# Softmax sums applied to the gates instead of to the exponentials, by way of DRAM, in a two-layer attention kernel

## The chip, the cores and the metric

The kernel runs on one core of one Trainium2 chip, in one launch. The metric is the device time of that launch in microseconds (us). A core has five engines that run side by side, each working through its own queue of instructions in a fixed order: TensorE (PE in the profile, with its weight loads listed apart as PEld), VectorE (DVE), ScalarE (ACT), GpSimd (POOL) and SyncE (SP), which here only issues DMA transfers. Engines wait for one another through semaphores. A result differs from "no change" here when it is more than 0.2% away.

## The reference

The reference is a trunk of two layers. Each layer normalises 512 latent tokens and 256 context tokens of width 1024, projects them with one combined weight `w_in`, runs two attention branches of eight heads of width 64, multiplies each branch by its own SiLU gate, and merges both branches. Branch A is a neighbourhood attention with a position bias, branch B a grouped-query attention. In layer 0 the context tokens are queries too (`first` in the kernel), in layer 1 only the latents are. What the change touches is this part, cut from the reference:

```python
def _attend(q, k, v):
    s = jnp.einsum('bqkgd,btkd->bkgqt', q, k).astype(jnp.float32) * (HEAD_DIM ** -0.5)
    p = jax.nn.softmax(s, axis=-1).astype(v.dtype)
    return jnp.einsum('bkgqt,btkd->bqkgd', p, v)

def _merge(a_att, b_att, a_z, b_z, g_a, g_b, w_o_a, w_o_b, w_out):
    o_a = (a_att * jax.nn.silu(a_z)) @ w_o_a
    o_b = (b_att * jax.nn.silu(b_z)) @ w_o_b
    merged = jax.nn.sigmoid(g_a) * o_a + jax.nn.sigmoid(g_b) * o_b
    return merged @ w_out
```

A softmax is an exponential divided by the sum of its row. The sum belongs to a query token, the output of a head is linear in the exponentials, and the output is multiplied by the gate of the same token. So the division can be made on the exponentials, on the head's output, or on the gate.

## The kernel before, in words

All inputs are float32. Each operand of a large product is split into a high and a low part and three products are summed, so a product of 128 by 512 by 1024 is 24 matmuls (`mm3`, lines 343 to 347). Weights come by DMA into three `raw` tiles, are copied on ACT to `whi` and subtracted on POOL or DVE to `wlo` (eight tiles of each).

A layer runs in this order: projections for branch A, branch A's attention (called NA here: neighbourhood attention), projections for branch B, branch B's attention (GQ: grouped-query attention), the merge. An attention is a loop over eight heads in `pipeline` (line 792). For head h it emits

1. the scores: q and k are staged (`stage_q`, and `stage_k` with its POOL subtraction at line 656), and for each of four tiles of 128 queries the score matmuls write PSUM (`pss`), DVE takes the row maximum (with the bias in NA, line 753; lines 685 and 899 elsewhere), ACT computes the exponential into a tile `p` and adds up its row into `r` (lines 756, 901, and 689 for context queries);
2. `softmax_tail` (line 605): a reciprocal of `r` on DVE (line 607), and the product of the whole `p` tile with 0.5/r, on DVE (line 610) for tiles 0 and 2 and the context tile, on POOL (lines 612 and 613) for tiles 1 and 3;
3. the values of head h-1: `transpose_split` (line 616) turns 128x128 blocks of `p` on TensorE into one of two PSUM tiles `pst`, ACT copies that to `pth` (line 626), DVE subtracts to `ptl` (line 627), and value matmuls add into the one PSUM tile `psv` (lines 776 to 787 in NA, 916 and 917 in GQ, 700 and 701 for context); `head_out` (line 630) adds the two halves of `psv` on ACT and DVE and multiplies the gate tile `za` or `zb` in place on POOL (line 637);
4. some pieces of `fill`: projections of gates and, in GQ, of branch A's output. They need nothing of the heads around them, so they give TensorE work while a head's softmax runs. In GQ all of them are emitted before the last head's values, in NA a ninth is left for after them.

Rows of the gate tile `za` (`zb`) hold channels: chunk j of the four has heads 2j on partitions 0 to 63 and 2j+1 on partitions 64 to 127, and tokens along the free axis. The factor 0.5 of the softmax belongs to the gate, which is kept as twice its SiLU.

`p` tiles come from a pool of 7 (NA, layer 0), 8 (NA, layer 1) or 10 (GQ) tiles, `NP_NA` and `NP_GQ`. Besides, both attentions of layer 0 and GQ of layer 1 have steps on DVE that work for a later modulation (`ada_steps`, line 223), a few per tile.

The order in which instructions stand on each engine is not that of the source: the program is built with a scheduler that follows the source's order where it can and moves an instruction ahead where its model of the engines says that the engine would idle. Only where `add_manual_dep` ties an instruction to the one emitted before it is this order kept. All DMA transfers of the kernel stand in one queue, SP's: one that waits holds up all behind it.

After GQ, branch B's gate tile is split again (`hilo`, line 516) and multiplied with `w_o_b`: chunks 0 to 2 early (`early`, line 928, one POOL subtraction each at line 520 into `gbl`), chunk 3 after the last head (line 948).

Of the kernel before, what the change touches and what calls it, by code (L numbers as in the profile page):

```python
# [28 lines left out]
NA_POOL = (1, 3)  # L29
GQ_POOL = (1, 3)  # L30
# [17 lines left out]
def hybrid_kernel(es: ExitStack, tc, x, ctx, cvec, w_ada, w_ada0, small, gvec, w_in, w_o_a, w_o_b, w_out,  # L48
                  bias_int, bias_edge, rope, ident_d, out):
    nc = tc.nc  # L50
# [46 lines left out]

    x0, ctx0 = x[0], ctx[0]
# [5 lines left out]
    cd = drp.tile([16, 128], F32, name="cd")  # L104
    gs = [drp.tile([128, 4, NTOK], F32, name=f"gs{c}") for c in range(4)]
# [95 lines left out]
    def ada_steps(l, tiles, halves, nv, pool):  # L201
# [13 lines left out]
        def dot(h, i, v):  # L215
            if v == 0:
                load_tile(h, i)
            w = cb["w"]
            o = w if v == nv - 1 else pool.tile([128, 512], BF16, tag="junk", name=nm("junk"), bufs=1)
            ins = nc.cur_bb.bb.instructions  # L220
            before = next(j for j in reversed(ins) if j.engine == mybir.EngineType.DVE)
            n = len(ins)
            V.tensor_tensor_reduce(o, w, cb[h][:, v, :], 1.0, 0.0, ALU.mult, ALU.add, asum[:, i, h, v:v + 1])
            for j in nc.cur_bb.bb.instructions[n:]:
                if j.engine == mybir.EngineType.DVE:
                    tc.add_manual_dep(j, before.name, mybir.DependencyInfo(
                        mybir.DependencyClass.NoSync, mybir.DependencyReason.DATA), reason="program order")
# [229 lines left out]
    def layer(l, hx, nxt, mid):  # L457
# [146 lines left out]
        if True:  # L604
            def softmax_tail(p, n, r, pieces, eng=None):

                V.reciprocal(r, r)  # L607
                for i, (c0, c1) in enumerate(pieces):
                    if eng is None:
                        V.tensor_scalar(p[:, c0:c1], p[:, c0:c1], r[:, i:i + 1], 0.5, ALU.mult, ALU.mult)  # L610
                    else:
                        G.tensor_scalar(r[:, i:i + 1], r[:, i:i + 1], 0.5, None, ALU.mult)  # L612
                        G.tensor_tensor(p[:, c0:c1], p[:, c0:c1],  # L613
                                        r[:, i:i + 1].to_broadcast([128, c1 - c0]), ALU.mult)
# [63 lines left out]
            def ctx_scores(q, kh, kl):  # L678
# [8 lines left out]
                r = sp.tile([128, 2], F32, tag="r", name=nm("r"), bufs=8)  # L687
                for i in range(2):
                    S.activation(p[:, 256 * i:256 * i + 256], pss[:, 256 * i:256 * i + 256], AF.Exp,
                                 bias=mx[:, i:i + 1], accum_out=r[:, i:i + 1])  # L690
                softmax_tail(p, 512, r, [(0, 256), (256, 512)])
# [41 lines left out]
            def na_scores(h, q, kh, kl):  # L733
# [354 lines left out]
```

## Time and profile before

| what | value |
|---|---|
| time, median of 3 runs | 1183.07 us (1182.45 to 1184.28) |
| the profiled execution, its own time | 1181.47 us |
| its span, first to last instruction | 1179.7 us |
| mean granted TensorE clock | 0.998 |
| NA of layer 0, then of layer 1, by the first and the last of their matmuls | 158 to 320 us, 805 to 917 us |
| GQ of layer 0, then of layer 1, likewise | 410 to 600 us, 968 to 1112 us |

The profile lists for each engine the busy time, and for each group of instructions the source line, the engine, the operation, the tile written and the tiles read (`ptl<-pst,pth`), the shape, the count, the busy time, the mean duration and the idle time of the engine just ahead of the group with what ended it. A matmul's duration is modelled and longer than the distance between two matmuls that follow each other, so a TensorE that is shown busy can still lose a little time.

### The profile page before, as it was taken

What the parts mean: (1) busy time and instruction counts of PE and PEld (TensorE: products, weight loads), DVE (VectorE), ACT (ScalarE), POOL (GpSimd) and SP (SyncE); (2) the same over time, 40 slices, a digit from 0 to 9 for tenths busy, and PEclk for the clock granted to TensorE, in tenths of its full rate; (3) what the DMA queues carried; (4) which work ended last, traced back from release to release, by engine and by line L of the source; (5) the groups of instructions that cost most, each with busy time, mean ns of one, the idle gap of its engine ahead of it and who ended that gap; (6) DMA issues with size and microseconds to landing.
All of it is one profiled execution on the core that took longest, in us unless ns stands there. A gap on an engine that the chain in (4) does not pass through costs nothing. (4 is left out here: it accounts for less than half of the span.)

```text
span 1179.7 us, 17337 instructions
## 1 busy us (share of the span) xinstructions
PE 1130.4 (96%) x6078; PEld 948.8 (80%) x6078; DVE 812.2 (69%) x1506; ACT 575.0 (49%) x1171; POOL 508.3 (43%) x463
## 2 busy tenths in 40 slices
PE   4999999899999999999999999999999999999898
PEld 3688877788897888878788887887888878877686
DVE  4476689987474499978683455339786757798573
ACT  4353255466453355566430355436666545756531
POOL 2362444453267233453420225336553764654311
PEclk9999999999999999999999999999999999999999
DMA  9544323422152343371170322312322525452133
GB/s 315 188 144 135 111 80 111 120 82 61 55 157 87 118 143 112 72 263 38 41 192 18 125 90 72 116 43 88 119 78 71 159 80 183 142 179 98 37 127 96
DMA packets 88128, 134.05 MB, mean 114 GB/s; under 512 B 10756, under 2 KB 52712, under 8 KB 86376
## 3 DMA queue, kind: packets, MB, share of 16 engines
q1 hardware_dynamic: 88040, 132.94, 36.1%
q8 instruction: 48, 0.79, 0.3%
q14 instruction: 40, 0.33, 0.1%
HBM read 115.58 MB, written 17.32 MB: 113 GB/s over the span
## 5 line engine op out<-in xcount | busy, mean ns | idle before, releaser
L627 DVE TENSOR_TENSOR ptl<-pst,pth 128x512 fp32r<-128x512 f32 (+1 forms) x176 | 115.9, 672 | 40.7 <-ACT pth L626 39.6
L332 POOL TENSOR_TENSOR wlo<-raw,whi 128x512 fp32r<-128x512 f32 x64 | 91.7, 1435 | 119.8 <-ACT whi L330 99.6
L345 PE MATMUL psf<-hx,whi 128*128 128x512 f32 (+1 forms) x368 | 138.9, 378 | 1.1 <-DVE za L480 1.0
L346 PE MATMUL psf<-hx,whi 128*128 128x512 f32 (+1 forms) x368 | 138.3, 376 | 0.0
L347 PE MATMUL psf<-hx,wlo 128*128 128x512 f32 (+1 forms) x368 | 137.9, 375 | 0.0
L626 ACT CAST pth<-pst 128x512 fp32r<-128x512 f32 (+1 forms) x176 | 98.8, 578 | 80.0 <-PE pst L623 56.2
L345 PE MATMUL psx<-whi,hx 128*128 128x512 f32 (+1 forms) x368 | 134.9, 374 | 0.0
L346 PE MATMUL psx<-wlo,hx 128*128 128x512 f32 (+1 forms) x368 | 134.4, 369 | 0.0
L347 PE MATMUL psx<-whi,hx 128*128 128x512 f32 (+1 forms) x368 | 133.4, 370 | 0.0
L318 POOL TENSOR_TENSOR wlo<-raw,whi 128x512 fp32r<-128x512 f32 (+1 forms) x52 | 68.1, 1310 | 146.1 <-ACT whi L315 123.6
L315 ACT CAST whi<-raw 128x512 fp32r<-128x512 f32 (+1 forms) x112 | 64.8, 591 | 111.2 <-PE psx L347 39.6
L330 ACT CAST whi<-raw 128x512 fp32r<-128x512 f32 x128 | 78.1, 621 | 56.2 <-DMA raw<-in_w_in_dram 41.0
L623 PE MATMUL pst<-ident,p 128*128 128x128 f32 x640 | 100.4, 273 | 3.6 <-POOL p L613 1.2
L623 PEld LDWEIGHTS pst<-ident,p 128*128 128x128 f32 x640 | 77.8, 140 | 16.8 <-POOL p L613 1.6
L613 POOL TENSOR_TENSOR p<-p,r 128x512 f32<-128x512 f32 (+1 forms) x64 | 86.6, 1353 | 5.2
L332 DVE TENSOR_TENSOR wlo<-raw,whi 128x512 fp32r<-128x512 f32 x64 | 63.4, 991 | 36.0 <-ACT whi L330 35.5
L612 POOL TENSOR_SCALAR r<-r 128x1 f32<-128x1 f32 x64 | 24.2, 378 | 135.9 <-DVE r L607 123.9
L345 PEld LDWEIGHTS psf<-hx,whi 128*128 128x128 f32 x368 | 69.5, 189 | 12.9 <-DVE za L480 1.7
L347 PEld LDWEIGHTS psx<-whi,hx 128*128 128x128 f32 x368 | 69.4, 189 | 12.0 <-issue 0.8
L345 PEld LDWEIGHTS psx<-whi,hx 128*128 128x128 f32 x368 | 70.0, 191 | 11.1
L346 PEld LDWEIGHTS psx<-wlo,hx 128*128 128x128 f32 x368 | 69.6, 189 | 11.3
L347 PEld LDWEIGHTS psf<-hx,wlo 128*128 128x128 f32 x368 | 69.4, 188 | 11.6
(239 smaller groups left out, 3049.4 us busy)
## 6 DMA issues: line engine op xcount, KB each, us to landing
raw<-in_w_in_dram SPq DMA_DIRECT2D x160, 256.0 KB, 2.9
rawb<-in_w_ada_dram SPq DMA_DIRECT2D x64, 256.0 KB, 2.7
gs<-zt SPq DMA_DIRECT2D x32, 256.0 KB, 2.6
raw<-in_w_out_dram SPq DMA_DIRECT2D x32, 256.0 KB, 2.7
tg<-gs SPq DMA_DIRECT2D x4, 1536.0 KB, 7.8
rawx<-in_w_ada_dram SPq DMA_DIRECT2D x4, 1024.0 KB, 11.9
rawy<-in_w_ada_dram SPq DMA_DIRECT2D x4, 1024.0 KB, 12.7
raw<-in_w_o_a_dram SPq DMA_DIRECT2D x16, 256.0 KB, 3.2
```

The lines of the kernel that those rows point to most:

```text
L315: S.copy(hi[:, :n], raw[:, :n])
L318: e.tensor_tensor(lo[:, :n], raw[:, :n], F(hi[:, :n]), ALU.subtract)
L330: S.copy(hi, raw)
L332: lo_eng(i).tensor_tensor(lo, raw, F(hi), ALU.subtract)
L345: T.matmul(ps, lhs[0], rhs[0], start=first, stop=False)
L346: T.matmul(ps, lhs[0], rhs[1], start=False, stop=False)
L347: T.matmul(ps, lhs[1], rhs[0], start=False, stop=last)
L612: G.tensor_scalar(r[:, i:i + 1], r[:, i:i + 1], 0.5, None, ALU.mult)
L613: G.tensor_tensor(p[:, c0:c1], p[:, c0:c1], r[:, i:i + 1].to_broadcast([128, c1 - c0]), ALU.mult)
L623: T.transpose(pt[:, c0:c0 + 128], src, ident)
L626: S.copy(hi[:, n0:n1], pt[:, n0:n1])
L627: V.tensor_tensor(lo[:, n0:n1], pt[:, n0:n1], F(hi[:, n0:n1]), ALU.subtract)
```

## The change: what it does

The exponentials are no longer divided. ACT still adds up each row, now into one tile `r` for a pair of heads: column pairs (query tile, head of the pair), 12 columns in layer 0, where the two context tiles count, and 8 in layer 1. After the odd head of a pair, `invert` doubles the sums and takes their reciprocal on DVE, and `sums_out` turns the 128x12 tile on TensorE into 12 rows of 128 in a `pst` tile, copies these on ACT into a `p` tile, and writes them to DRAM (`rd`). During the next head, `normalise` reads the rows back, each spread over the 64 partitions of its head (two transfers, one for each half of the partitions), into one or two `p` tiles, and multiplies chunk j of the gate tile with them on POOL. In NA the tile is 512 wide, so in layer 0 there are two such tiles, and the latents' part is multiplied in two pieces, because its first query tile is made of two pieces of 64 tokens. For the last pair this stands ahead of the values of head 7. The new helper `behind` ties what it emits to the instruction emitted last on the same engine; the writes of the sums and the first three `normalise` of an attention are emitted through it, so that the scheduler does not move them ahead of what the source has before them. `softmax_tail` and the two constants that chose its engine go.

```diff
+    def behind(fn):
+        ins = nc.cur_bb.bb.instructions
+        n, last = len(ins), {}
+        for i in ins[::-1]:
+            last.setdefault(i.engine, i.name)
+            if len(last) == 5:
+                break
+        fn()
+        for i in nc.cur_bb.bb.instructions[n:]:
+            if i.engine in last:
+                tc.add_manual_dep(i, last[i.engine], mybir.DependencyInfo(
+                    mybir.DependencyClass.NoSync, mybir.DependencyReason.DATA), reason="program order")
+            last[i.engine] = i.name
...
+    rd = [drp.tile([12, 128], F32, name=f"rd{i}") for i in range(4)]
...
-            def softmax_tail(p, n, r, pieces, eng=None):
-                V.reciprocal(r, r)
-                for i, (c0, c1) in enumerate(pieces):
-                    if eng is None:
-                        V.tensor_scalar(p[:, c0:c1], p[:, c0:c1], r[:, i:i + 1], 0.5, ALU.mult, ALU.mult)
+            def sums_tile():
+                return sp.tile([128, 6, 2], F32, tag="r", name=nm("r"), bufs=3)
+
+            def invert(r):
+                n = 6 if first else 4
+                V.tensor_scalar(r[:, 0:n], r[:, 0:n], 2.0, None, ALU.mult)
+                V.reciprocal(r[:, 0:n], r[:, 0:n])
+
+            def sums_out(j, r):
+                n = 12 if first else 8
+                pt = psw(128, "t")
+                T.transpose(pt[0:n], r[:, 0:n // 2].rearrange("p j e -> p (j e)"), ident)
+                row = p_tile()[:, 0:128]
+                S.copy(row[0:n], pt[0:n])
+                behind(lambda: nc.sync.dma_start(rd[j][0:n], row[0:n]))
+
+            def normalise(j, z, perm):
+                zv = z.rearrange("p (f n) -> p f n", f=4)[:, j]
+                n = 6 if first else 4
+                w = min(att["w"] // 128, n)
+                for j0 in range(0, n, w):
+                    j1 = min(j0 + w, n)
+                    rb = p_tile()[:, 0:128 * (j1 - j0)]
+                    for e in range(2):
+                        nc.sync.dma_start(rb[64 * e:64 * e + 64].rearrange("p (j q) -> p j q", q=128),
+                                          rd[j].rearrange("(j e) q -> e j q", e=2)[e:e + 1, j0:j1]
+                                          .to_broadcast([64, j1 - j0, 128]))
+                    if perm and j0 == 0:
+                        zp = zv[:, 0:512].rearrange("p (s n) -> p s n", n=64)[:, 0:8:7]
+                        G.tensor_tensor(zp, zp, rb[:, 0:128].rearrange("p (s n) -> p s n", n=64), ALU.mult)
+                        G.tensor_tensor(zv[:, 64:448], zv[:, 64:448], rb[:, 128:512], ALU.mult)
                     else:
-                        G.tensor_scalar(r[:, i:i + 1], r[:, i:i + 1], 0.5, None, ALU.mult)
-                        G.tensor_tensor(p[:, c0:c1], p[:, c0:c1],
-                                        r[:, i:i + 1].to_broadcast([128, c1 - c0]), ALU.mult)
+                        zp = zv[:, 128 * j0:128 * j1]
+                        G.tensor_tensor(zp, zp, rb, ALU.mult)
...
                     S.activation(p[:, :512], p[:, :512], AF.Exp, bias=mx[:, 0:1], scale=-1.0,
-                                 accum_out=r[:, 0:1])
-                    softmax_tail(p, 512, r[:, 0:1], [(0, 512)], G if i in NA_POOL else None)
+                                 accum_out=r[:, i, h % 2:h % 2 + 1])
...
+            def pair_sums(h):
+                if h % 2 == 0:
+                    att["r"] = sums_tile()
+                return att["r"]
+
-            def pipeline(fill, spread, scores_of, values_of, last=None, bg=[]):
+            def pipeline(fill, spread, scores_of, values_of, z, perm, last=None, bg=[]):
...
                     if prev is not None:
                         values_of(h - 1, prev)
+                    if h % 2:
+                        invert(att["r"])
+                        sums_out(h // 2, att["r"])
+                    elif h:
+                        behind(lambda: normalise(h // 2 - 1, z, perm))
                     run(fill, len(fill) - (n - n * min(h + 1, spread) // spread))
...
                 run(bg, len(bg))
+                normalise(3, z, perm)
                 values_of(7, prev)
```

The same replacement of `softmax_tail` by a column of `r` is made in `ctx_scores` and `gq_scores`. The old inline tie in `ada_steps` now goes through `behind`.

More of the change, by code (lines that the diff above doesn't have):

```diff
@@ L219, in dot @@
             o = w if v == nv - 1 else pool.tile([128, 512], BF16, tag="junk", name=nm("junk"), bufs=1)
[L220 to L227, printed above, removed]
+            behind(lambda: V.tensor_tensor_reduce(o, w, cb[h][:, v, :], 1.0, 0.0, ALU.mult, ALU.add,
+                                                  asum[:, i, h, v:v + 1]))
         res = []
```

31 lines of the change are left out of this document (13 added, 18 removed).

## The prediction

> **What bounds the kernel now.** I read the head of the page first, then the busy time by stage, then who waits for whom on PE, then single waits on the timeline.
>
> ```profile
> span 1179.7 us, 17337 instructions
> PE 1130.4 (96%) x6078; PEld 948.8 (80%) x6078; DVE 812.2 (69%) x1506; ACT 575.0 (49%) x1171; POOL 508.3 (43%) x463
> ```
>
> TensorE is busy for 96% of the span, and none of its matmuls is removed. So the change can only buy back time in which TensorE waits, 1179.7 - 1130.4 = 49.3 us in all, and of that only what lies in the four attentions. The busy time by stage gives that part (the columns are PE, PEld, DVE, ACT and POOL, each with its count, then PE's clock, the DMA share and GB/s); the rows are NA and GQ of layer 0, then NA and GQ of layer 1:
>
> ```profile
> 158.00:320.00 162.00, 154.24 (x948) 135.67 (x949) 135.69 (x302) 90.06 (x206) 72.12 (x64) 1.00 0.29 87
> 410.00:600.00 190.00, 184.70 (x1116) 160.59 (x1115) 158.47 (x290) 107.75 (x223) 82.97 (x69) 1.00 0.40 120
> 805.00:917.00 112.00, 110.58 (x609) 94.06 (x608) 89.37 (x182) 73.09 (x156) 57.98 (x59) 1.00 0.28 89
> 968.00:1112.00 144.00, 138.31 (x708) 111.26 (x707) 114.66 (x200) 88.79 (x170) 67.52 (x58) 1.00 0.42 136
> ```
>
> TensorE idles 7.76 + 5.30 + 1.42 + 5.69 = 20.2 us there. This is a little low, because a matmul's row overlaps the next: starts 0.23 us apart, shown as 0.39 us each, so every wait hides up to 0.16 us.
>
> ```profile
> 1110.93 0.39 PE L345 MATMUL psx<-gbh,whi 128*128 128x512 f32 x1
> 1111.16 0.39 PE L346 MATMUL psx<-gbl,whi 128*128 128x512 f32 x1
> ```
>
> Some 30 such waits would add 5 us; 25 us is the ceiling. NA of layer 0 is the one place where another engine is as full as TensorE:
>
> ```profile
> 158.00:178.00 20.00, 17.94 (x108) 15.39 (x108) 18.97 (x42) 10.73 (x26) 9.19 (x7) 1.00 0.29 91
> 178.00:198.00 20.00, 19.15 (x107) 16.25 (x108) 19.87 (x49) 10.95 (x26) 8.79 (x7) 1.00 0.36 95
> 198.00:218.00 20.00, 18.43 (x119) 16.40 (x118) 19.87 (x43) 10.30 (x25) 9.83 (x8) 1.00 0.36 119
> 218.00:238.00 20.00, 16.73 (x101) 14.40 (x100) 19.43 (x41) 10.67 (x25) 9.55 (x7) 1.00 0.44 132
> 238.00:258.00 20.00, 20.00 (x128) 17.95 (x128) 18.60 (x44) 12.78 (x30) 11.91 (x10) 1.00 0.31 96
> ```
>
> DVE works 96.7 of these 100 us, and TensorE loses 7.75 us, all the idle time of that stage. Who ended it, in the same stretch (us in total, times, longest):
>
> ```profile
> PE pst L621 <- DVE ptl L627: 4.8, 2, 3.3
> PE pss L672 <- DVE za L480: 1.3, 1, 1.3
> ```
>
> **Removed.** The groups of the page (mean ns after the busy time):
>
> ```profile
> L610 DVE TENSOR_SCALAR p<-p,r 128x512 f32<-128x512 f32 (+2 forms) x96 | 64.3, 683 | 2.8 <-PE pst L623 0.5
> L607 DVE RECIPROCAL r<-r 128x1 f32<-128x1 f32 (+1 forms) x144 | 21.8, 156 | 11.9 <-ACT p L901 5.4 <-ACT p L756 4.6 <-ACT p L689 1.3
> L613 POOL TENSOR_TENSOR p<-p,r 128x512 f32<-128x512 f32 (+1 forms) x64 | 86.6, 1353 | 5.2
> L612 POOL TENSOR_SCALAR r<-r 128x1 f32<-128x1 f32 x64 | 24.2, 378 | 135.9 <-DVE r L607 123.9
> ```
>
> DVE loses 86 of 812 us, POOL 111 of 508. Nearly all of it lies beside a busy TensorE and is worth nothing by itself. Stage by stage:
>
> *NA, layer 0.* Of DVE's 96.7 us in the full stretch these two groups go:
>
> ```profile
> L610 DVE TENSOR_SCALAR p<-p,r 128x512 f32<-128x512 f32 (+1 forms) x18 | 11.4, 652 | 0.1
> L607 DVE RECIPROCAL r<-r 128x1 f32<-128x1 f32 (+1 forms) x24 | 3.6, 154 | 0.3 <-ACT p L756 0.3
> ```
>
> That is 15.0 us, twice what TensorE loses, so DVE is no longer the last on average. The wait for `za` (1.3 us) is not touched. The longest one, 3.3 us, has a cause that partly stays:
>
> ```profile
> 228.35 2.48 POOL L656 TENSOR_TENSOR kl<-ka,kh 64x768 fp32r<-64x768 f32 x1 [1.31 <-DVE kh L654]
> 229.20 2.18 DVE L223 CUSTOM_DVE_ANT_0 rawb<-rawb,cb 128x512 f32<-128x512 f32 x1
> 232.05 0.33 PE L621 MATMUL pst<-ident,p 128*128 128x128 f32 x1 [3.27 <-DVE ptl L627]
> ```
>
> The subtraction `ptl` sat behind a DVE step that took 2.18 us while POOL was working; both remain. I take 5.0 us off; bounds 0 and 9.0 (7.75 - 1.3, with 2.5 for hidden parts).
>
> *GQ, layer 0*, 5.30 us idle. Two stretches hold 4.26 of it:
>
> ```profile
> 510.00:530.00 20.00, 17.71 (x106) 14.77 (x105) 17.73 (x28) 13.14 (x28) 14.74 (x11) 1.00 0.95 365
> 570.00:590.00 20.00, 18.03 (x113) 15.22 (x112) 11.18 (x17) 7.73 (x14) 10.58 (x8) 1.00 0.13 47
> ```
>
> In the first the DMA engines are 95% busy, in the second every engine is idle half the time: neither lacks DVE. I take 1.0 us; bounds 0 and 3.0.
>
> *NA, layer 1*: 1.42 us idle; 0.5, bounds 0 and 1.4. *GQ, layer 1*: 3.16 of its 5.69 us lie at the end, where the last three heads run without fill and each group of four transposes goes through ACT and DVE before the next may start. The first and the last of ten `ptl` there:
>
> ```profile
> 1098.70 0.69 DVE L627 TENSOR_TENSOR ptl<-pst,pth 128x512 fp32r<-128x512 f32 x1 [0.49 <-ACT pth L626]
> 1109.85 0.69 DVE L627 TENSOR_TENSOR ptl<-pst,pth 128x512 fp32r<-128x512 f32 x1 [0.45 <-ACT pth L626]
> ```
>
> 11.15 us for nine, 1.24 us a group: no division stands in this chain any more, and it stays. Of the other 2.5 us I take 1.0; bounds 0 and 2.5. Saved together: 5.0 + 1.0 + 0.5 + 1.0 = 7.5 us; bounds 0 and 15.9.
>
> **Added.** Sixteen times (four pairs, two attentions, two layers): two DVE operations on 12 columns, less than the four or five reciprocals a head loses; one transpose on TensorE; one ACT copy of 12 rows; one DMA write of 4 or 6 KB; 40 DMA reads; POOL products in the place of four times as many.
>
> The transpose: a run of four takes 0.60 us, a run's first 0.27 by its group's mean, so (0.60 - 0.27) / 3 = 0.11 us each.
>
> ```profile
> L623 PE MATMUL pst<-ident,p 128*128 128x128 f32 x640 | 100.4, 273 | 3.6 <-POOL p L613 1.2 <-DVE ptl L627 1.2 <-DVE p L610 0.7
> 1108.60 0.60 PE L623 MATMUL pst<-ident,p 128*128 128x128 f32 x4
> ```
>
> Sixteen are 1.8 us; at 0.27 each, if none overlaps, 4.4. I take 1.8: fill stands around most of them. Each also borrows one of the two `pst` tiles. Under fill that is covered; in the bare ends of layer 1's attentions it costs about half a group, 0.6 us, twice: 1.2 us, from 0 to 2.5.
>
> The way through DRAM shows in no row of before. Nearest are the gates written and the `cb` rows read with a spread over partitions (first line: `zs`; second: `cb`; min, median, max); then a short copy on ACT and the issue of a transfer on SP:
>
> ```profile
> DMA to landing us min/median/max: 1.7/2.3/6.7
> DMA to landing us min/median/max: 3.1/3.6/5.1
> L635 ACT COPY ho<-psv 64x256 f32<-64x256 f32 x16 | 5.9, 368 | 10.1 <-PE psv L701 4.6 <-POOL zb L637 3.1 <-POOL za L637 2.2
> 1109.15 0.33 SPq L973 DMA_DIRECT2D xt<-xs  x1
> ```
>
> With ACT's copy (0.37 us for 256 columns), two issues of 0.33 us and the POOL product (1.35) I get 0.4 + 0.3 + 2.3 + 0.3 + 3.6 + 1.35 = 8.3 us; at the fastest rows 7.2, at the slowest 14.2. What hides it is that for three pairs of four a whole head lies between; what is queued behind it is everything on SP behind the write (weight loads, kept ahead by eight `whi`) and everything on POOL behind the product. In the built program the `kl` behind it on POOL serves a score more than a hundred matmuls later. The cover is thin for the last pair of each GQ. In layer 0 the order on POOL puts the product ahead of three `gbl`; TensorE's transpose of the sums stands right behind head 6's values:
>
> ```profile
> 571.20 0.48 PE L917 MATMUL psv<-ptl,vb 128*128 128x512 f32 x1
> 580.42 5.88 POOL L520 TENSOR_TENSOR gbl<-zb,gbh 128x768 fp32r<-128x768 f32 x3 [3.60 <-PE psf L346]
> ```
>
> From 571.4 to 580.4 are 9.0 us, against 8.3. In layer 1 six groups follow the transpose (7.4 us) and then
>
> ```profile
> 1110.60 0.50 PE L917 MATMUL psv<-ptl,vb 128*128 128x512 f32 x1 [0.23 <-DVE ptl L627]
> 1112.57 1.29 POOL L637 TENSOR_TENSOR zb<-zb,ho 64x512 f32<-64x512 f32 x1 [6.04 <-DVE ho L636]
> ```
>
> another 2.0 us until POOL needs the gate: 9.4 us, against 8.3. I cost the round trip at 0; at the slowest rows it is 14.2 - 9.0 = 5.2 us late once and 4.8 us once, 10 us. The `p` tiles that row and product borrow are given back within these 8 us; in NA of layer 0, with seven, this makes the scheduler place a score later, with fill ahead of it: nothing, as long as fill lasts.
>
> Sum: -7.5 + 1.8 + 1.2 = -4.5 us on the span, 1175.2. The profiled execution took 1181.47 against a median of 1183.07, so I carry the difference to the median: 1178.6 us.
>
> **The rivals.**
>
> *A. The round trip comes late* (slower). Place: POOL at the end of GQ in layer 0 and layer 1, where `gbl` and the last gate products queue behind a product that waits for DRAM. It costs from the point where copy, write, read and product pass 9 us; at 14.2 us it costs 10 us, so 1178.6 + 10 = 1188.6. For it: a write of `zs` took 6.7 us once. Against it: DMA is 13% busy in the stretch of layer 0's end.
>
> *B. TensorE's waits stay.* The scheduler fills the room that DVE gains: in the built order the third head of NA in layer 0 ends 36 projection matmuls earlier in TensorE's queue than before, so attention work comes denser and DVE may be last again. Then nothing is saved and 3.0 us are added: 1186.1 us. Against it: by the sixth head both orders are even, and by then DVE has shed more than the 15 us above.
>
> *C. DVE gains more than its removed rows.* DVE lines with two operands in SBUF, such as line 223, run long at times; for this line the count with its mean and then min, median and max in ns:
>
> ```profile
> L223 DVE CUSTOM_DVE_ANT_0 rawb<-rawb,cb 128x512 f32<-128x512 f32 x64 | 59.0, 922 | 1.2 <-DMA rawb<-in_w_ada_dram 0.6
> L223 DVE CUSTOM_DVE_ANT_0 rawb<-rawb,cb x64: 662/691/2183, 98.8 to 1045.3; 128x512 f32<-128x512 f32 x64
> ```
>
> The mean is 922 ns (59.0 us for 64), 231 ns over the median, and the 2.18 us row above ran beside a POOL operation. If POOL's load is the cause, losing 111 of its 508 us, less some 35 for the new products, shortens these steps by about 15%. Then the long waits of NA go too: 7.75 - 1.3 there, and half of the remaining 12.4 us elsewhere: -12.7 + 3.0 = -9.7, 1173.4 us. [...]
>
> **How the numbers follow.** The forecast 0.40, A 0.23, B 0.22, C 0.15. The bound for no change is 0.2%, 2.4 us. The forecast's own range (its savings between 3 and 11 us, 3.0 added) is 1175 to 1183. Its 0.40 goes 0.33 faster, 0.06 the same, 0.01 slower; C is all faster; A 0.03 the same, 0.20 slower; B 0.10 the same, 0.12 slower, as 3.0 lies near the bound. Faster 0.48, same 0.19, slower 0.33. The range takes in all savings at their bound less the additions (1183.1 - 15.9 + 1.8 = 1169) and A at its full price with a third of the savings lost (1191).
>
> **What would show it.** Right: PE idle in 158 to 258 us down from 7.75 to about 3, DVE there below 85%; sixteen transposes near 0.11 us; PE's order of stages unchanged; POOL's product of the last pair done before `gbl`'s turn. Wrong: PE waits for `gbl` or a last gate product at the end of GQ with a DMA as releaser (A); PE idle in NA of layer 0 still above 6 us (B); `rawb` steps near 700 ns (C). A TensorE wait for the transposed sums themselves, behind DVE's reciprocal, would be a cost that I left out.

## The result, and the profile after

The changed kernel takes 1185.69 us (median of 20 runs, 1183.18 to 1188.0), the kernel before 1183.1 us in as many runs beside it. The ratio is 1.0024 with an interval of 1.0017 to 1.0031: 2.6 us slower, where 1178.6 was forecast. The profiled execution took 1184.74 us.

The head of the page of the changed kernel:

```profile
span 1182.8 us, 17163 instructions
PE 1133.9 (96%) x6094; PEld 952.8 (81%) x6094; DVE 733.1 (62%) x1298; ACT 580.3 (49%) x1187; POOL 419.6 (35%) x363
```

DVE lost 79 us, where 86 of removed rows were counted, and POOL 89, where 111 less some 35 were. TensorE idles 1182.8 - 1133.9 = 48.9 us, before 49.3: nothing in sum. Its busy time is 3.5 us longer with the same matmuls and sixteen transposes. The busy time by stage (window and length, then PE, PEld, DVE, ACT and POOL with counts, PE's clock, DMA share, GB/s):

```profile
158.00:258.00 100.00, 98.36 (x606) 86.90 (x607) 85.44 (x181) 59.55 (x133) 32.55 (x24) 1.00 0.38 117
158.00:320.00 162.00, 160.36 (x1001) 142.29 (x1001) 116.22 (x241) 94.79 (x217) 54.09 (x46) 1.00 0.33 101
410.00:600.00 190.00, 186.70 (x1133) 163.16 (x1132) 134.79 (x227) 107.25 (x222) 59.75 (x42) 1.00 0.40 127
805.00:917.00 112.00, 108.89 (x620) 93.82 (x619) 72.78 (x144) 69.92 (x152) 42.85 (x38) 0.98 0.31 95
968.00:1112.00 144.00, 132.59 (x674) 106.02 (x673) 94.97 (x154) 83.88 (x164) 39.44 (x30) 0.99 0.42 130
```

TensorE's idle time in NA and GQ of layer 0 falls from 7.76 and 5.30 us to 1.64 and 3.30, and in NA and GQ of layer 1 rises from 1.42 and 5.69 to 3.11 and 11.41: 8.1 us won, 7.4 lost. The clock column, 1.00 in all four stages before, shows 0.98 and 0.99 in layer 1.

The same on the timeline: the last value matmuls of GQ in layer 0, of NA in layer 1 and of GQ in layer 1, first in the kernel before, then in the changed one (start, duration):

```profile
584.38 0.48 PE L917 MATMUL psv<-ptl,vb 128*128 128x512 f32 x1
...
913.32 0.25 PE L787 MATMUL psv<-ptl,va 128*128 128x192 f32 x1
```

```profile
574.97 0.48 PE L958 MATMUL psv<-ptl,vb 128*128 128x512 f32 x1
...
906.88 0.25 PE L818 MATMUL psv<-ptl,va 128*128 128x192 f32 x1
...
1113.74 0.50 PE L958 MATMUL psv<-ptl,vb 128*128 128x512 f32 x1 [0.23 <-DVE ptl L662]
```

The changed kernel is 9.4 us ahead after layer 0's attentions, 6.4 ahead after NA of layer 1, and 3.1 behind at the end of GQ of layer 1 (1113.74 against 1110.60). That last attention loses 9.6 us. Three places in the trace of the changed kernel stand out there.

*The first step on `w_ada`.* The start of GQ in layer 1 on DVE, SP, ACT and PE, then DVE and ACT at the same place before (start, duration, engine, instruction, idle time ahead of it and what ended it):

```profile
965.87 0.96 DVE L942 TENSOR_REDUCE mx<-pss 128x1 f32<-128x768 f32 x1 [0.33 <-PE pss L708]
969.43 0.84 DVE L234 CUSTOM_DVE_ANT_0 rawb<-rawb,cb 128x512 f32<-128x512 f32 x1 [2.61 <-DMA rawb<-in_w_ada_dram]
970.21 0.95 DVE L942 TENSOR_REDUCE mx<-pss 128x1 f32<-128x768 f32 x1
...
970.31 1.80 SPq L227 DMA_DIRECT2D rawb<-in_w_ada_dram  x2
972.21 1.61 SPq L335 DMA_DIRECT2D raw<-in_w_in_dram  x2
...
976.48 0.62 ACT L338 CAST whi<-raw 128x512 fp32r<-128x512 f32 x1 [3.27 <-DMA raw<-in_w_in_dram]
977.01 0.59 ACT L486 ACTIVATE zt<-psf 128x512 f32<-128x512 f32 x1
977.65 0.50 PE L353 MATMUL psf<-hx,whi 128*128 128x512 f32 x1 [3.81 <-ACT zt L486]
```

```profile
972.27 1.82 DVE L899 TENSOR_REDUCE mx<-pss 128x1 f32<-128x768 f32 x2 [0.34 <-PE pss L673]
974.29 0.17 DVE L607 RECIPROCAL r<-r 128x1 f32<-128x1 f32 x1 [0.20 <-ACT p L901]
974.49 0.62 DVE L610 TENSOR_SCALAR p<-p,r 128x768 f32<-128x768 f32 x1
975.72 1.09 DVE L223 CUSTOM_DVE_ANT_0 rawb<-rawb,cb 128x512 f32<-128x512 f32 x1 [0.61 <-DMA rawb<-in_w_ada_dram]
...
978.46 0.60 ACT L478 ACTIVATE zt<-psf 128x512 f32<-128x512 f32 x1 [0.96 <-PE psf L347]
980.86 0.62 ACT L330 CAST whi<-raw 128x512 fp32r<-128x512 f32 x1 [1.80 <-DMA raw<-in_w_in_dram]
```

The step is tied to the DVE instruction emitted last before it. Before, that was the division, which waits for the exponential: two row maxima passed ahead of it and its tile had nearly landed. Now it is the first row max. The step sits in DVE's queue 2.61 us for its transfer, with the second row max behind it. SP waits with it, for a free `rawb` buffer, so the next weight tile is asked for only at 972.21; ACT waits for that tile in front of `zt`, and TensorE for the PSUM tile that `zt` reads, 3.81 us.

SP's wait alone does not make this loss. In the kernel before SP stood still for as long (from 972.2 to 976.84), and TensorE had no such wait. Two more things differ. Two loads of `w_ada` now go ahead of the weight tile, where one did before, and ACT's cast comes 10.6 us after the first row max instead of 8.6. And `zt` now stands on ACT behind the cast that waits; before it stood ahead of it (978.46, then 980.86). Both are parts of the new order, and no run takes them apart.

*The doubling of the sums.* POOL, DVE and PE in the last heads:

```profile
1098.67 1.28 POOL L672 TENSOR_TENSOR zb<-zb,ho 64x512 f32<-64x512 f32 x1 [9.66 <-DVE ho L671]
1098.70 1.27 DVE L619 TENSOR_SCALAR r<-r 128x8 f32<-128x8 f32 x1
1100.01 0.20 DVE L620 RECIPROCAL r<-r 128x8 f32<-128x8 f32 x1
1100.24 1.29 DVE L662 TENSOR_TENSOR ptl<-pst,pth 128x512 fp32r<-128x512 f32 x2
1100.99 0.50 PE L958 MATMUL psv<-ptl,vb 128*128 128x512 f32 x1 [1.28 <-DVE ptl L662]
```

Eight columns take 1.27 us; they end when POOL's product ends, and `ptl` and TensorE wait behind them.

*The store of the gate sums.* It goes to DRAM as single numbers, and here it stands right ahead of two weight loads:

```profile
1043.63 0.37 SPq L256 DMA_DIRECT2D gd<-ag  x1
1044.09 2.12 SPq L335 DMA_DIRECT2D raw<-in_w_o_b_dram  x2
...
1056.44 0.62 ACT L338 CAST whi<-raw 128x512 fp32r<-128x512 f32 x1 [4.79 <-DMA raw<-in_w_o_b_dram]
1057.60 0.50 PE L957 MATMUL psv<-pth,vb 128*128 128x512 f32 x1 [1.46 <-ACT pth L661]
```

ACT waits 4.79 us for a weight tile that was issued by 1046.2, with `pth` behind it.

The round trip itself, for the last pair of GQ in layer 1 on SP and POOL:

```profile
1105.49 0.29 SPq L629 DMA_DIRECT2D rd<-p  x1
1106.85 1.23 SPq L640 DMA_DIRECT2D p<-rd  x2
1110.85 1.28 POOL L649 TENSOR_TENSOR zb<-zb,p 128x512 f32<-128x512 f32 x1 [1.17 <-DMA p<-rd]
```

From the write's issue to the end of the product are 6.64 us, and the last value matmuls end only after 1113.74.

### The profile page after: what moved, and what is told of

Its sections match the earlier page's. It is cut to its first block, busy times and chain, and to the rows that moved or that the text cites. A ratio compares the mean times of both kernels' runs of the same rounds, so it can differ in the third digit from the quotient of the medians.

```text
span 1182.8 us, 17163 instructions
## 1 busy us (share of the span) xinstructions
PE 1133.9 (96%) x6094; PEld 952.8 (81%) x6094; DVE 733.1 (62%) x1298; ACT 580.3 (49%) x1187; POOL 419.6 (35%) x363
## 4 chain that ended last, share of the span: by engine, by line
PE 72%; DVE 10%; POOL 6%; DMA 5%; ACT 3%; issue 3%; SPq 0%; DVEq 0%; POOLq 0%; ACTq 0%
PE psx L353 10%; PE psx L354 10%; PE psx L355 10%; PE psf L353 8%; PE psf L354 8%; PE psf L355 8%; PE pst L658 4%; DMA raw<-in_w_in_dram 2%; PE pss L707 2%; PE pss L708 2%; PE pss L783 1%; PE psv L958 1%; POOL rsb L264 1%; DVE ptl L662 1%; PE psv L957 1%
## 5 line engine op out<-in xcount | busy, mean ns | idle before, releaser
L340 POOL TENSOR_TENSOR wlo<-raw,whi 128x512 fp32r<-128x512 f32 x64 | 88.6, 1387 | 203.4 <-ACT whi L338 172.1
L340 DVE TENSOR_TENSOR wlo<-raw,whi 128x512 fp32r<-128x512 f32 x64 | 59.8, 934 | 49.6 <-ACT whi L338 49.1
L353 PEld LDWEIGHTS psf<-hx,whi 128*128 128x128 f32 x368 | 69.8, 190 | 19.1 <-ACT zt L486 5.1
L354 PEld LDWEIGHTS psf<-hx,whi 128*128 128x128 f32 x368 | 69.8, 190 | 10.5
L942 DVE TENSOR_REDUCE mx<-pss 128x1 f32<-128x768 f32 x64 | 60.6, 949 | 26.7 <-PE pss L708 26.6
```

The source lines that it names most:

```text
L340: lo_eng(i).tensor_tensor(lo, raw, F(hi), ALU.subtract)
L353: T.matmul(ps, lhs[0], rhs[0], start=first, stop=False)
L354: T.matmul(ps, lhs[0], rhs[1], start=False, stop=False)
L942: V.tensor_reduce(mx[:, 0:1], pss, AX, ALU.max, negate=True)
```

## The experiments

The theory to test (Theory 1): layer 1's loss comes from the order in its GQ, above all from the step on `w_ada` that the division no longer holds back. Its main rival: the round trip through DRAM. Each row of this table has the median of a kernel, that of the kernel before in runs beside it, and the ratio of the two, which is taken from the single runs and not exactly the quotient of the medians. "Under" and "over" before are differences of the medians.

| kernel | us | before, us | ratio (95%) |
|---|---|---|---|
| changed | 1185.69 | 1183.10 | 1.0024 (1.0017 to 1.0031) |
| e1_late_ada | 1180.33 | 1183.91 | 0.9970 (0.9958 to 0.9982) |
| e2_no_trip | 1188.49 | 1183.91 | 1.0041 (1.0027 to 1.0056) |
| e3_old_gq1 | 1178.30 | 1183.91 | 0.9947 (0.9933 to 0.9960) |
| e4_only_gq1 | 1192.77 | 1183.91 | 1.0079 (1.0067 to 1.0092) |
| e5_act_half | 1176.37 | 1183.48 | 0.9935 (0.9923 to 0.9947) |
| e6_dot_later | 1182.15 | 1183.48 | 0.9989 (0.9978 to 0.9999) |
| e7_old_l1 | 1175.20 | 1183.48 | 0.9927 (0.9915 to 0.9939) |
| e8_before_early | 1188.22 | 1183.48 | 1.0038 (1.0025 to 1.0051) |
| e9_na1_old | 1175.88 | 1183.68 | 0.9933 (0.9921 to 0.9945) |
| e10_no_turn | 1177.69 | 1183.68 | 0.9952 (0.9939 to 0.9966) |
| e11_twice | 1179.95 | 1183.68 | 0.9966 (0.9953 to 0.9978) |
| e12_only_half | 1185.00 | 1183.20 | 1.0014 (1.0003 to 1.0024) |
| e13_gd_late | 1185.10 | 1183.61 | 1.0013 (1.0000 to 1.0026) |
| e14_three | 1178.40 | 1183.61 | 0.9959 (0.9946 to 0.9971) |

**Where the loss is.** In e3 the division of before stands in GQ of layer 1 alone, in e7 in both attentions of layer 1; e4 is the reverse of e3, the new division in that one attention of the kernel before. The edit, with the condition of e3 (`name == "gq1"` in e4, `l == 0` in e7):

```diff
+                att["new"] = name != "gq1"
...
+                    if ro is not None:
+                        softmax_tail(p, 768, ro[:, 0:1], [(0, 768)], G if i in DIV_POOL else None)
```

> The changed kernel, except that layer 1's grouped attention alone divides as before (reciprocal and scale of each score tile on VectorE and GpSimd, no transposed sums, no round trip). Theory 1 (the loss arises inside that attention, and the 6 us by which the changed kernel enters it early are real): before less 5 to 8 us, 1175 to 1178, ratio 0.993 to 0.996. Theory 3 (the lead is taken back whoever divides, because a bound further on, such as the DMA traffic or the granted clock, holds the end): 1181 to 1185, ratio 0.998 to 1.002.

> The kernel before, with the new division in layer 1's grouped attention alone. Theory 1 (the loss arises inside that attention whatever the lead on entering it): before plus 6 to 10 us, 1189 to 1193, ratio 1.005 to 1.009. Theory 3 (the lead of the other three attentions is what is taken back, by a bound further on): before plus 0 to 3 us, ratio 1.000 to 1.003.

> The changed kernel in layer 0, the division of before in both attentions of layer 1. Theory 1a (layer 1's neighbourhood attention loses 2 to 3.5 us too, as its last value matmuls stand 9.4 us early at its start and 6.4 at its end): 1173 to 1176 us, ratio to before 0.991 to 0.9935. Rival (layer 1's neighbourhood attention is neutral, the 3 us are the measure's): as e3, 1177.5 to 1179.5, ratio 0.994 to 0.996.

Both e3 (5.6 us under before) and e4 (8.9 over) came out as Theory 1 has it: GQ of layer 1 costs 8 to 9 us by itself, whatever lead it is entered with. Layer 0's new division is worth 8.3 us (e7), and NA of layer 1 seemed to cost about 2.7 (e7 against e3, each by its own before; their intervals overlap).

**The step on `w_ada`, or the round trip.** e1 starts the steps in GQ of layer 1 with the second head:

```diff
                 for h in range(8):
+                    att["bg"] = bg if h >= first_bg else []
                     st = scores_of(h)
...
-            pipeline(fill, 8, gq_first, values_of(zb, gq_values), zb, False, early, bg)
+            pipeline(fill, 8, gq_first, values_of(zb, gq_values), zb, False, early, bg, 1 * l)
```

> The changed kernel, except that layer 1's grouped attention starts the steps on w_ada (rawb times cb, on VectorE) with its second head instead of its first. Theory 1 (the first such step now stands ahead of the second row max in VectorE's queue while its tile is still on the way, because the division that used to stand between them is gone; by this the PE wait of 3.8 us that ends at 977.65 comes about, and the granted clock of 0.5 from 978.8 to 982.2 behind it): that wait falls under 1 us and the dip behind it goes, 4 to 6 us in all: 1179.5 to 1182 us, against 1185.7 for the changed kernel, ratio to before 0.997 to 0.999. Theory 2 (the round trip through DRAM is what costs): the first heads have no round trip, so the time stays within 1 us of 1185.7, ratio 1.0015 to 1.003.

e2 keeps every instruction, but in GQ of layer 1 no read waits for a write of the same head pair (`trip` is set in that attention alone):

```diff
-                behind(lambda: nc.sync.dma_start(rd[j][0:n], row[0:n]))
+                behind(lambda: nc.sync.dma_start((rx if att["trip"] else rd)[j][0:n], row[0:n]))
```

> The changed kernel, except that in layer 1's grouped attention the turned sums are written to a DRAM tile that nothing reads, and the factors are read from what layer 1's neighbourhood attention left (the output is not the reference's there: it is divided by other sums). Every instruction and transfer stays, only the wait of the reads for the write is gone. Theory 1 (order of VectorE's queue in the first heads): within 1 us of the changed kernel's 1185.7, ratio to before 1.0015 to 1.003. Theory 2 (the round trip, Rival A of the prediction): 3 to 9 us less, ratio 0.995 to 0.9995.

e1 gains 6.2 us on the changed kernel (3.6 under before against 2.6 over), e2 none: it came out about 2 us above, which nobody expected and which lies at the edge of the two intervals. The round trip of that attention is not the loss. In e1's trace the wait at that place is down to 0.87 us:

```profile
973.92 0.50 PE L353 MATMUL psf<-hx,whi 128*128 128x512 f32 x1 [0.87 <-ACT zt L486]
```

**Its place in the queue, in both kernels.** e6 leaves the loads where they are and puts each step behind the next row max. e8 does the reverse to the kernel before: the step ahead of the division, nothing else.

```diff
+            def shift(h, i):
+                load_tile(h, i)
+                todo.append((h, i, 0, cb["w"]))
+                if len(todo) > 1:
+                    dot(*todo.pop(0))
...
```

```diff
                     S.activation(p, pss, AF.Exp, bias=mx[:, 0:1], accum_out=r[:, 0:1])
+                    if l == 1:
+                        run(att["bg"], att["per"])
                     softmax_tail(p, 768, r[:, 0:1], [(0, 768)], G if i in GQ_POOL else None)
                     ps_.append(p)
-                    run(att["bg"], att["per"])
+                    if l == 0:
+                        run(att["bg"], att["per"])
```

> The changed kernel, with each step on w_ada in layer 1's grouped attention put one score tile later in VectorE's order, so behind the next row max; the loads of its tiles are issued in the same heads as in the changed kernel. Theory 1 (the step's place in VectorE's queue is what costs): about what e1 gains, 1179.5 to 1182.5 us, ratio to before 0.997 to 0.9995. Rival (the traffic of these loads in the first head costs, wherever the step stands): within 1.5 us of 1185.7, ratio 1.0010 to 1.0035.

> The kernel before, with nothing changed but that in layer 1's grouped attention each step on w_ada is placed ahead of the division of its score tile instead of behind it, so that it stands behind the first row max in VectorE's order as in the changed kernel. Theory 1 (that place is what costs): before plus 3 to 6 us, 1186.5 to 1190, ratio 1.0025 to 1.005. Rival (the place costs nothing by itself; the loss needs the new division's other parts): within 1.2 us of before, ratio 0.999 to 1.001.

e8 makes the kernel before 4.7 us slower without a single part of the change, and its trace shows the row that the changed kernel has:

```profile
974.26 0.96 DVE L899 TENSOR_REDUCE mx<-pss 128x1 f32<-128x768 f32 x1 [0.34 <-PE pss L673]
977.72 0.94 DVE L223 CUSTOM_DVE_ANT_0 rawb<-rawb,cb 128x512 f32<-128x512 f32 x1 [2.50 <-DMA rawb<-in_w_ada_dram]
978.59 0.95 DVE L899 TENSOR_REDUCE mx<-pss 128x1 f32<-128x768 f32 x1
```

Where TensorE pays for it is not all the same, though. It waits 1.30 us for `zt` here (at 984.92), 1.76 for `ptl` at 1051.47, and two stretches at half clock follow in this attention, from 1052.09 and 1103.29 (see the last section). So e8 shows that the order costs, not that it always costs by one wait.

e6 gains 3.9 us of e1's 6.2 (1.3 under before against 2.6 over), at the far end of what Theory 1 gave; TensorE still waits 2.05 us at that place:

```profile
979.02 0.50 PE L366 MATMUL psf<-hx,whi 128*128 128x512 f32 x1 [2.05 <-ACT zt L499]
```

So the place in the queue is most of it. The rest, 2.3 us, e6 does not divide: the loads are still issued in the first head, and `zt` still stands behind the cast that waits.

**The doubling.** e5 is e1 without line 619; the factor goes into ACT's copy. e12 is the same edit on the changed kernel, without e1's.

```diff
-                V.tensor_scalar(r[:, 0:n], r[:, 0:n], 2.0, None, ALU.mult)
...
-                S.copy(row[0:n], pt[0:n])
+                S.activation(row[0:n], pt[0:n], AF.Identity, scale=0.5)
```

> The kernel of e1_late_ada, with the doubling of the sums on VectorE (L619) dropped; ScalarE halves the turned reciprocals in the copy that it makes anyway. In e1's trace L619 of the last pair takes 1.27 us at 1091.62 and ends with POOL's product (L672, 1091.59 to 1092.87), beside 0.16 us where POOL is idle, and ptl of the value matmuls stands behind it. Theory A (that instruction waits for POOL's product, and TensorE for it): 1 to 2 us less than e1's 1180.3, so 1178.3 to 1179.5, ratio to before 0.9950 to 0.9963. Rival (the reciprocal inherits the wait, or ScalarE's pth is as late): within 0.5 us of e1, ratio 0.9965 to 0.9980.

> The changed kernel with one edit: the doubling of the sums on VectorE (L619) is dropped, and ScalarE halves the turned reciprocals in its copy. The w_ada steps stay where the changed kernel has them. e5 against e1 puts this edit at 4 us (1176.4 against 1180.3) where the trace of e1 shows one instruction of 1.27 us and one of 0.76. Theory A (the two faults add up: each holds up its own place): 1181 to 1183 us, ratio to before 0.998 to 1.000. Rival (the wait for w_ada's tile and the clock behind it hide it, or most of the 4 us was the later start's): 1184 to 1186, ratio 1.001 to 1.003.

On e1 the edit gains 3.5 us (7.1 under before against 3.6), more than Theory A had. TensorE's idle time in GQ of layer 1 falls from 7.61 to 5.78 us between the two traces, which is half of that; where the other half lies was not settled. The reciprocal does not inherit the wait. In e5's trace it takes 0.20 us while POOL's product runs (it is line 619 here, since a line above it is gone):

```profile
1091.85 1.28 POOL L671 TENSOR_TENSOR zb<-zb,ho 64x512 f32<-64x512 f32 x1 [9.66 <-DVE ho L670]
1091.88 0.20 DVE L619 RECIPROCAL r<-r 128x8 f32<-128x8 f32 x1
1093.11 0.50 PE L958 MATMUL psv<-ptl,vb 128*128 128x512 f32 x1 [0.23 <-DVE ptl L661]
```

On the changed kernel itself the edit gains only 0.8 us (1.8 over before against 2.6), with overlapping intervals, as the rival had it: the two faults do not add up. In e12's trace the wait for `zt` is still there, now 4.08 us at 978.04. The wait for `ptl` is gone, but the one for `pth` behind the store of the gate sums is 2.12 us (at 1058.58) instead of 1.46, and a stretch at half clock follows from 1059.81, where the changed kernel's trace has none. In this one execution these two cost more than the wait that is gone; whether it is so in the others no run shows.

**NA of layer 1 again.** e9 is e5 with the division of before in that attention.

```diff
+                att["new"] = name != "na1"
```

> The kernel of e5_act_half (later start of the w_ada steps, halving on ScalarE), with the division of before in layer 1's neighbourhood attention, the new one in the other three. Theory 1a (the new division loses 2 to 3 us in that attention, as e3 against e7 has it): 1173 to 1174.5 us where e5 has 1176.4, ratio to before 0.9905 to 0.9925. Rival (e3 and e7 differ by something else; with the halving on ScalarE the loss there is gone): as e5, ratio 0.993 to 0.9945.

The rival held: 7.8 us under before against 7.1, within the intervals. With the halving on ACT the new division costs nothing in NA of layer 1 that the time shows. What the 2.7 us between e3 and e7 are stays open. Line 619 took 0.74 us in NA's last pair in the changed kernel. But TensorE also waits there for `ptl`, 0.73 us at 894.26, and for the head's output:

```profile
897.02 0.79 PE L807 MATMUL psv<-pth,va 128*128 128x512 f32 x1 [1.41 <-DVE ho L671]
```

Both end before line 619 starts (897.61), both are as long in e5's trace (at 895.55 and 898.31), where that line is gone, and neither is in e9's. TensorE's idle time from 805 to 917 us says the same: 3.11 us in the changed kernel, 3.21 in e5, 1.42 in e9 and in the kernel before.

**The turning of the sums, and the slack of the round trip.** e10 drops the transposes, the copies and the writes; e11 sends the rows over a second DRAM tile. Both start from e5.

```diff
             def sums_out(j, r):
+                return
...
```

```diff
-                behind(lambda: nc.sync.dma_start(rd[j][0:n], row[0:n]))
+                behind(lambda: nc.sync.dma_start(rx[j][0:n], row[0:n]))
+                behind(lambda: nc.sync.dma_start(rd[j][0:n], rx[j][0:n]))
...
```

> The kernel of e5_act_half without the turning of the sums: no transposes of them, no ScalarE copy of the rows, no write; the reads take rows that were put into the DRAM tiles once in layer 0 from x, so zb and za are multiplied by other numbers than the reference's. The reciprocals, reads and products stay. By the prediction's terms (1.8 us for the transposes, 1.2 for the borrowed pst tile) it gains 3.0 us: 1172.5 to 1174.5, ratio to before 0.9905 to 0.9925. Rival (both lie in TensorE's waits in the bare ends and cost nearly nothing): within 1 us of e5's 1176.4, ratio 0.9925 to 0.9945.

> The kernel of e5_act_half with the round trip made longer by one hop: the row is written to a second DRAM tile, and from there copied to the one that is read. That is some 1.5 to 3.5 us more by the traces (write to read issue took 1.36 us for the last pair of layer 0's grouped attention in the changed kernel's trace, 3.46 in e6's). Theory (the trip only just fits: in e6's trace POOL waited 3.70 us for the read there and TensorE 2.07 behind it, in the changed kernel's 1.80 and none): 1 to 5 us more than e5's 1176.4, ratio to before 0.9945 to 0.998. Rival (the cover is far longer than the trip): within 0.8 us of e5, ratio 0.993 to 0.9943.

e10 does not give the price of the transposes. It came out 1.1 us above e5 (6.0 under before against 7.1, within the intervals) instead of 3 below. Its trace is better in one layer and worse in the other. In GQ of layer 0, which the scheduler orders in another way without the transposes, TensorE idles 6.99 us, in e5 3.41:

```profile
410.00:600.00 190.00, 183.01 (x1093) 158.28 (x1093) 128.38 (x210) 104.69 (x215) 57.69 (x41) 0.99 0.39 124
```

In layer 1 it idles less than in e5: 1.60 us against 3.21 in NA, 3.62 against 5.78 in GQ, 3.8 in sum. That is the size of the 3.0 us of the forecast's terms, but from one execution and in another order. e11 costs 3.4 us (3.7 under before against 7.1), as expected if the trip only just fits. The place is the end of GQ in layer 0, POOL and PE in e11's trace:

```profile
570.03 1.84 POOL L650 TENSOR_TENSOR zb<-zb,p 128x768 f32<-128x768 f32 x1 [4.10 <-DMA p<-rd]
574.14 0.50 PE L355 MATMUL psf<-gbl,whi 128*128 128x512 f32 x1 [2.28 <-POOL gbl L529]
```

The extra hop isn't needed for that. With the same trip at this place POOL waited 1.80 us in the profiled execution of the changed kernel, 3.70 in that of e6 and 3.62 in that of e13, and in the last two TensorE waited behind it, 1.87 us (where the expectation has 2.07) and 1.79. e6's rows:

```profile
572.06 1.83 POOL L662 TENSOR_TENSOR zb<-zb,p 128x768 f32<-128x768 f32 x1 [3.70 <-DMA p<-rd]
576.16 0.50 PE L367 MATMUL psf<-gbl,whi 128*128 128x512 f32 x1 [1.87 <-POOL gbl L541]
```

**The store of the gate sums.** e13 holds the gate step back by six score tiles; e14 has this (by five, as e6's order takes one itself), e6's order and e5's halving together, without e1's later start.

```diff
-            bg = ada_steps(l, range(16, 24), (0, 1), nv, att["p"]) + [lambda: ada_gate(l, nv)]
+            bg = (ada_steps(l, range(16, 24), (0, 1), nv, att["p"]) + [lambda: None] * (6 * l)
+                  + [lambda: behind(lambda: ada_gate(l, nv)) if l else ada_gate(l, nv)])
```

> The changed kernel, in which layer 1's gate step (ada_gate, with the store gd<-ag) is held back by six score tiles; the steps on w_ada stay in place. In the changed kernel's trace that store is issued at 1043.63, right ahead of two loads of in_w_o_b; one of these lands after 11.2 us, ScalarE waits 4.79 us for it in front of whi (1056.44), and TensorE 1.62 us at 1057.60. In e1 the store stands at 1060.83, with no load of in_w_o_b behind it for 5 us. Theory 4 (that store is a second part of what e1's later start moved): the ScalarE wait and the TensorE wait at 1057 go, 2 to 4 us less than 1185.7, so 1181.5 to 1184, ratio to before 0.9985 to 1.0005. Rival (e1's whole gain lies in the first heads, at 977): within 1 us of the changed kernel, ratio 1.0016 to 1.0032.

> The changed kernel with the three edits together and without e1's later start: each w_ada step one score tile later on VectorE (e6), the gate step held back (e13), the halving on ScalarE (e5). If these three are what the prediction missed in layer 1: 1175.5 to 1178, ratio to before 0.9930 to 0.9955, as e5. Rival (the later start of the loads was worth something by itself): 1179 to 1182, ratio 0.996 to 0.999.

e13's gain is 1.1 us, between what the two sides expected, and its interval reaches into both; the wait at 1057 (1.46 us in the row above, where the expectation has 1.62) is gone from its trace, but the 4.51 us for `zt` at 981.39 are there. e14 reaches 5.2 us under before, 1.9 short of e5: just above what was given for the three edits, and just under what the rival gave. So the later start of the loads may be worth something too; the intervals of e14 and e5 only touch. The wait for `zt` is 2.31 us in its trace.

## Why the prediction was wrong

*NA and GQ of layer 0, -6.0 us: right in mechanism, too small.* The two attentions came out 9.4 us ahead on the timeline, and 8.3 in e7. TensorE's idle time from 158 to 258 us went from 7.75 to 1.64 us (about 3 was named), with DVE at 85.4%.

*GQ of layer 1, -1.0 us with bounds 0 and -2.5: this step failed.* It costs 8 to 9 us (e3, e4). The working asked only which of TensorE's waits there the division causes, and found none that it makes worse. It did not ask what the division held back. The `w_ada` steps are tied to the instruction emitted before them; with the division gone that is an instruction 2 to 3 us earlier on DVE, while their tiles come no earlier. The bound at 0 excluded a loss without a reason given. e8 shows that this place alone costs 4.7 us; e1 shows 6.2 us for taking the steps out of the first head, of which e6 leaves 3.9 to the place in DVE's queue. How the rest divides between the loads, the order on ACT and the store of the gate sums stays open. Nor did the working count the clock: TensorE's busy time was taken as fixed, and it grew by 3.5 us.

*"Two DVE operations on 12 columns, less than the four or five reciprocals a head loses": this step failed too.* True of their busy time with POOL idle (0.16 us), not beside a POOL product, where it takes 1.27 us, and that in the bare end where the prediction itself had counted each group of the chain. The cost that it named as possibly left out, a TensorE wait behind DVE's work on the sums, is this one, though it fell on `ptl` and not on the transpose. Taking line 619 away is worth 3.5 us once the steps are out of the way (e5), 0.8 alone (e12), which is within the noise. In NA of layer 1, forecast at -0.5, TensorE's idle time rose by 1.7 us and stays as high without line 619 (e5), so there this line is at most a part of the loss.

*Added, 1.8 + 1.2 us:* not measured by e10's time, since the order changes with it. In the changed kernel's trace each of the sixteen transposes shows as 0.27 us, not 0.11. TensorE's busy time, though, is 1130.0 us in e1's trace, with them, and 1130.4 before, without.

*The round trip at 0:* right for the changed kernel's traced execution, and e2 gains nothing without it in GQ of layer 1. There it took 6.64 us from the write's issue, where the estimate has 7.9 without ACT's copy. The estimate of 8.3 us for 9.0 of cover was close to the edge, and e11 shows it: a hop more costs 3.4 us. Rival A did happen at its first place, in the executions profiled for e6 and e13, at 2 us rather than 5.

*Rival B* is refuted: TensorE's waits in NA of layer 0 went. That its 1186.1 us lies next to the measured time is chance. *Rival C* was partly right. The `rawb` steps fell by 14%, where 15% was worked out:

```profile
L234 DVE CUSTOM_DVE_ANT_0 rawb<-rawb,cb 128x512 f32<-128x512 f32 x64 | 50.7, 792 | 3.1 <-DMA rawb<-in_w_ada_dram 2.6
```

In the kernel before 39 of these 64 steps ran beside an instruction on POOL, 1072 ns on the mean, and 25 with POOL idle, 686 ns; in the changed kernel 18 and 46, with 1073 and 682 ns. TensorE's waits, though, did not go down as the rival has it: they fell in layer 0 only. The idle time in that row, 2.6 us for a transfer, is nearly all the wait of that one step in GQ of layer 1 (2.61 us).

With both faults mended the new division is 7.1 us faster than before (e5), where the prediction's sum was -4.5. The division of before in all of layer 1 is as fast (e7, 8.3 us), and so is the mended kernel with the old division in NA of layer 1 alone (e9, 7.8): their intervals overlap, all three are faster than both kernels of the study.

## What to carry to other kernels

Before removing work from an engine's queue, list what is tied behind it and what transfers that follower waits for: removed work may have been the pause in which a load landed, as with the first step here. Price a small new instruction by what the neighbouring engine does at that moment, as with the doubling, and put it on an engine that is not in the chain. And take no bound at zero for a stage whose order a scheduler will make anew.

## What the hardware showed

*A wait paid twice, by the clock.* Inside the attentions the granted clock drops at times to 0.50, for 3.41 us. The two drops of the changed kernel start 81.93 us apart (896.90 and 978.83), 24 times 3.41, and the two of e8 in GQ of layer 1 51.20 us (1052.09 and 1103.29), 15 times 3.41: they fit one grid per execution. Busy time by the stretches of such a grid, two places of the changed kernel, then one of e1 with the first pair's wait at another place of its grid (the clock is the last column but two):

```profile
893.49:896.90 3.41, 1.39 (x11) 1.11 (x10) 2.64 (x7) 3.36 (x8) 0.00 (x0) 1.00 0.00 0
896.90:900.31 3.41, 3.29 (x11) 2.80 (x12) 2.12 (x5) 1.07 (x4) 2.69 (x3) 0.50 0.00 0
...
975.42:978.83 3.41, 1.18 (x5) 1.00 (x6) 1.70 (x3) 1.72 (x4) 0.00 (x0) 1.00 0.55 175
978.83:982.24 3.41, 3.41 (x10) 2.62 (x9) 2.63 (x6) 1.88 (x4) 0.00 (x0) 0.50 0.68 193
982.24:985.65 3.41, 3.41 (x19) 2.87 (x18) 0.00 (x0) 0.58 (x1) 0.00 (x0) 1.00 0.20 74
```

```profile
895.22:898.63 3.41, 1.89 (x10) 1.38 (x10) 3.26 (x7) 2.31 (x6) 2.03 (x3) 1.00 0.00 0
898.63:902.05 3.42, 2.53 (x19) 2.11 (x19) 1.78 (x3) 2.08 (x5) 0.68 (x1) 1.00 0.03 6
```

TensorE was busy 1.39 and 1.18 of 3.41 us ahead of the two drops, 1.89 in e1, where none followed. In the second drop it shows 10 matmuls, in the stretch behind it, as full, 19. By an estimate from these rows each drop costs half a stretch, 1.7 us, since TensorE was busy through nearly all of both; two would make 3.4 of the 3.5 us by which its busy time grew (1130.4 us at a mean clock of 0.998 before, 1133.9 at 0.995 in the changed kernel). The traces fit this roughly: e1, e5, e7 and e9, with no drop in their attentions, have 1130.0 to 1132.8 us of TensorE time at a mean clock of 0.997 or 0.998, e2 with two 1134.4 at 0.995, e8 with three 1135.4 at 0.993. The limit is not sharp: 1.63 us at 230.27 in the kernel before brought no drop, 1.65 at 1048.69 in e8 did.

*A 128x8 instruction on DVE held up by POOL.* Line 619, with its minimum, median and maximum in ns in the changed kernel:

```profile
L619 DVE TENSOR_SCALAR r<-r x16: 156/171/1272, 186.0 to 1098.7; 128x12 f32<-128x12 f32 x8, 128x8 f32<-128x8 f32 x8
```

Ten of the sixteen ran with POOL idle and took 156 to 174 ns. The other six began beside a product on POOL, took 229 to 1272 ns and ended within 0.05 us of the end of that product, wherever in it they began. The reciprocal of the same columns took 185 to 228 ns in all sixteen cases, seven of them beside POOL. Why the one waits and the other does not, no trace here shows.

*A store of single numbers, and the load issued behind it.* In layer 1 of the kernel before `gd<-ag`, 4 KB as 1024 numbers, landed after 11.8 us. In the changed kernel a weight tile of 256 KB took 11.2 us right behind that store, with the DMA engines 24 to 44% busy from 1046 to 1058 us and moving 14 and 15 GB/s up to 1054; the tiles of `w_in`, of the same size, land in 2.8 us (median), the sixteen of `w_o_b` in 7.8, and in 3.1 in the kernel before. In e13, where the store comes later, ACT has no such wait in front of `whi` (1055.22).
